# Other durations in the planner that orders attention, the entry of the output projection and the entry of the feed forward

## The chip, the cores and the metric

One core of a Trainium2 chip runs the whole kernel. The metric is the device time of one execution in microseconds (us), from three runs. Engines are named as in the profile: PE is TensorE (PEld its weight loads), DVE is VectorE, ACT is ScalarE, POOL is GpSimd, SP issues DMAs.

## The reference

One step of a backbone over 512 latent tokens (a grid of 8 x 64) and 128 context tokens of width 2048, all in float32:

```
m = silu(cond) @ w_ada + b_ada                      # shift, scale, gate, twice
h = rms_norm(x) * (1 + scale) + shift
q, k, v, u = split(h @ w_in)                        # 8 heads x 128 for q, k, v; 1024 for u
attn = softmax(q_n . [k_n in an 8 x 16 window + bias ; all 256 cached keys]) @ [v ; cached v]   # latent
attn = softmax(q_n . k_n) @ v                                                                   # context
pool = (window mean(u, 2/4/8/16) - u) @ w_pool * pool_scale
x = x + gate * concat(rms_norm(attn), rms_norm(pool)) @ w_out
h = rms_norm(x) * (1 + scale) + shift
x = x + gate * (silu(h @ w_gate) * (h @ w_up)) @ w_down
```

q_n and k_n are RMS-normalised per head. The outputs are both x and the context's k_n and v.

## The kernel before, in words

**Products.** Every large product is made of 256 x 256 blocks of weights, multiplied with seven products where the plain way has eight (a Strassen-Winograd form). The 640 tokens are two halves of 320 (`HB`; 322, `HX`, in the feed forward, where two columns carry the shift). One operand is a pair of 128-row tiles of activations, the other a 256 x 256 block of weights; of each, four given quarters and sums of them make seven tiles. Each tile is split into a high part (`hi`, rounded to the format that PE takes at full rate) and a low part (`lo`, the rest), so one of the seven products is three matmuls (lines 415 to 417). A **step** is one block of weights against one operand: 7 x 3 matmuls. Eight steps fill seven PSUM banks, and `combine` (lines 422 and 423; the first instruction is a ScalarE copy) adds them into an output block.

**What a step needs.** Its block of weights is fetched (`fetch`, line 336), its sums are made by three subtractions or additions (`sums`, line 342: 128, 128 and 256 columns), ScalarE copies the seven tiles to `hi` (`x_hi`, line 351), and a subtraction gives `lo` (`x_lo`, line 357, 896 columns). The operand of activations needs the same once: sums (`y_sum`, line 376: 640, 320 and 320 columns), copies to `hi` on ScalarE (lines 387 and 394), and subtractions for `lo` (line 389, 960 columns; line 396, 640 columns, twice).

**Who sets the order.** In most of the kernel the order stands in the loops (`step`): sums on GpSimd, `lo` on VectorE. In three stretches a planner sets it: the first block of the input projection, attention with the first block of the output projection, and the last block of the output projection with the first block of the feed forward. Code there records operations with `op` or `on`; each has a key (when it is wanted), a list of what it needs, the buffers it takes, and a duration for each engine that may do it. `issue` then lists them: it keeps a clock for each engine, computes for each operation that can be placed when it could start, takes the engine with the least start plus weighted duration, and among all that could start within a small window of the earliest places the one with the least key. The order in which operations are placed is the order in which each engine's instructions stand in the program; the engines wait for each other by semaphores, so the planner's clock is not seen at run time. The durations come from

```
    COST = {"ACT": (0.15, 0.83e-3), "DVE": (0.08, 1.05e-3), "Pool": (0.15, 2.1e-3)}
    ...
            fixed, each = (0.15, 0.65e-3) if copy and e == "DVE" else COST[e]
            alts[e] = fixed + each * n
    ...
                    (max(t, clock.get(e, 0.0)) + d * (1.0 + WEIGHT.get(e, 0.0)), max(t, clock.get(e, 0.0)), e)
```

(lines 530 to 540 and the choice in `issue`; `n` is the number of columns, the result is in us), and `STEP = 2.83` is the duration of a step on PE and the distance between the keys of two steps. `WEIGHT` makes VectorE and ScalarE count dearer in that choice than their durations say; the change leaves it alone.

**Attention** (lines 853 to 1476) records eight heads of five query blocks each. A block's chain is: scores on PE (lines 1069 to 1072), bias added on VectorE in PSUM (1080; the bias itself, masked, is made by line 1056 on VectorE or GpSimd), maximum (1093, 1094, VectorE), exponential (1100, ScalarE), reciprocal (1112, VectorE), transposes (1117, PE), a copy out of PSUM (544 ScalarE or 546 VectorE), values (1127, PE), a scaled copy (544 or 548). Beside it run the pooled features (`plan_features`, lines 1225 to 1249, elementwise on VectorE or GpSimd; products at 1269; their squares added at 1302), copies of x (1442), and the eight operands of the output projection: four of the pooled features (scaled at 1367) and, once all heads are done, four of attention (the sum over heads at 1397, its power at 908, a diagonal at 912, a row at 1329, scaled at 1419).

**The entry of the feed forward** (lines 1600 to 1730) records the last block of the output projection, the update of x (1507), its squares (1526, 552, 554, added at 1519 and 1627), the row of its norm (1329), and the eight operands of the feed forward.

Of the kernel before, what the change touches and what calls it, by code (L numbers as in the profile page):

```python
# [49 lines left out]
def tile_hybrid_step(  # L50
# [36 lines left out]
    def pool(name, **kw):  # L87
        cm = tc.tile_pool(name=name, bufs=1, reuse_waits="tile", **kw)
        return cm, cm.__enter__()
# [12 lines left out]
    def c_tile(i):  # L102
        return cp.tile([P, 2 * HX], F32, tag=f"c{i}", name=f"c{i}", bufs=1)
# [356 lines left out]
    def kind(name, n, make, begin=0.0):  # L460

        makers[name], held[name] = make, [begin] * n
# [4 lines left out]
    def op(eng, dur, key, fn, after=(), uses=(), lat=0.0):  # L467

        o = SimpleNamespace(eng=eng, dur=dur, key=key, fn=fn, after=[a for a in after if a], uses=uses, lat=lat, end=None)
        for b in uses:  # L470
            b.users.append(o)
        plan.append(o)
        return o
# [6 lines left out]
    def issue(begin=None, window=0.25):  # L480

        clock = dict(begin or {})
        taken.clear()
        plan.sort(key=lambda o: o.key)
        while plan:
            ready = []
            for o in plan:
                if any(a.end is None for a in o.after):
                    continue
                t = max([0.0] + [a.end + HOP for a in o.after])  # L490
                wanted = {}
                for b in o.uses:
                    if b.tile is None:
                        wanted.setdefault(b.kind, []).append(b)
                for k, bs in wanted.items():
                    t = max(t, sorted(free_at(h) for h in held[k])[len(bs) - 1])
                if t > 1e8:
                    continue
                alts = o.eng if isinstance(o.eng, dict) else {o.eng: o.dur}
                _, t, eng = min(  # L500
                    (max(t, clock.get(e, 0.0)) + d * (1.0 + WEIGHT.get(e, 0.0)), max(t, clock.get(e, 0.0)), e)
                    for e, d in alts.items()
                )
                ready.append((t, o, wanted, eng, alts[eng]))
            first = min(r[0] for r in ready)
            t, o, wanted, eng, dur = min((r for r in ready if r[0] <= first + window), key=lambda r: r[1].key)
            for k, bs in wanted.items():
                for b in bs:
                    i = min(range(len(held[k])), key=lambda i: free_at(held[k][i]))
                    held[k][i] = b  # L510
                    b.tile = makers[k](i)
            o.fn(eng) if isinstance(o.eng, dict) else o.fn()
            clock[eng] = t + dur
            o.end = t + dur + o.lat
            plan.remove(o)
# [16 lines left out]
    COST = {"ACT": (0.15, 0.83e-3), "DVE": (0.08, 1.05e-3), "Pool": (0.15, 2.1e-3)}  # L532
# [23 lines left out]
    STEP = 2.83  # L556
# [289 lines left out]
    def slot_tile(i, part, dtype):  # L846
        hop = hopA if i < 4 else hopB
        return hop.tile([P, 7 * HX], dtype, tag=f"{part}{i}", name=f"y{part}{i}", bufs=1)
# [3 lines left out]

    att_cm, att = pool("att")
    ps_cm, psum = pool("att_ps", space=PSUM)
    LEAD = 10.0

    att_kinds = set()

    def sb_kind(name, shape, n):
        att_kinds.add(name)  # L860
        kind(name, n, lambda i: att.tile(shape, F32, tag=f"{name}{i}", name=f"{name}{i}", bufs=1), LEAD)

# [28 lines left out]
    for name, n in (("s", 2), ("tp", 2), ("o", 1), ("x", 3), ("y", 0)):  # L891
        att_kinds.add(name)
        kind(name, n, lambda i, name=name: psum.tile([P, 512], F32, tag=f"{name}{i}", name=name, bufs=1), LEAD)

# [33 lines left out]

    begin = op("none", 0.0, -99, lambda: None, (), (), LEAD)
    later = op("none", 0.0, -99, lambda: None, (), (), 60.0)  # L930
# [258 lines left out]
    work = [[slot_tile(i, n, F32) for n in ("hi", "lo")] for i in range(2)]  # L1189
    kind("wk", 2, lambda i: work[i], LEAD)  # L1190
    SH = EXT + EXP
# [241 lines left out]
    kind("xi", 1, lambda i: c_tile(1)[:, 0:512])  # L1433
    kind("xo", 1, lambda i: c_tile(3)[:, 0:512], LEAD + 9)

# [54 lines left out]
    WEIGHT.update(DVE=1.6, ACT=0.5)  # L1490
    issue({e: LEAD for e in ("PE", "ACT", "DVE", "Pool")}, 0.05)
    c = [c_tile(q) for q in range(2)]
# [500 lines left out]
```

## Time and profile before

| what | us |
|---|---|
| median of 3 runs (2791.48 to 2798.62) | 2794.66 |
| the profiled execution | 2795.32 |
| its span, first to last instruction | 2793.1 |
| busy in the span: PE / DVE / ACT / POOL | 2616.0 / 1882.4 / 1087.4 / 1970.8 |
| from the last combine of the input projection to the first of the output projection | 569.65 to 807.00 |
| from the sixth further combine to the first of the feed forward | 968.41 to 1066.38 |

The profiled execution's time is 2.2 us above its span. An engine's busy time is from the start to the end that the record of an instruction shows, so time in which a running instruction is held up counts as busy. "Idle before" names what ended an engine's wait. A granted clock of 1.0 is PE's upper level (2.4 GHz), 0.5 its lower (1.2 GHz).

### The profile page before, as it was taken

To read this page: it belongs to the slowest core of one execution; us is meant where nothing else is said; L and a number is where in the kernel's file an instruction comes from. 1 tells how busy PE (TensorE), PEld (TensorE's weight loads), DVE (VectorE), ACT (ScalarE), POOL (GpSimd) and SP (SyncE) were. 2 spreads that over 40 slices of the span, in tenths; PEclk is the share of its full clock that TensorE was granted. 3 is DMA by queue.
4 is the path that set the end of the run, shared out by engine and by line. 5 is a ranking of instruction groups with operands and counts; after the bars stand their busy time and mean duration, and the time that the engine had idled before them with its cause. 6 is when DMAs were issued, how large, how long until landed. Compare 5 with 4: busy or idle time off the path is not lost.

```text
span 2793.1 us, 46356 instructions
## 1 busy us (share of the span) xinstructions
PE 2616.0 (94%) x16936; PEld 2424.4 (87%) x16936; DVE 1882.4 (67%) x2578; ACT 1087.4 (39%) x1605; POOL 1970.8 (71%) x2244
## 2 busy tenths in 40 slices
PE   6998999988779968999999999999999899999998
PEld 2478888877679968998999999999999889999997
DVE  2486434358775697665777777777777667787776
ACT  3133223246533434343444444444444323333333
POOL 2255656657678877666888888888888646887874
PEclk9999999989989979999999999999999999999999
DMA  9935777677245444664344344443443775365353
GB/s 333 340 120 205 270 252 260 229 228 221 84 142 177 158 134 137 201 193 141 117 126 144 122 135 122 126 140 117 126 140 115 260 250 206 127 211 190 111 168 103
DMA packets 370677, 487.17 MB, mean 174 GB/s; under 512 B 22928, under 2 KB 286608, under 8 KB 369808
## 3 DMA queue, kind: packets, MB, share of 16 engines
q1 hardware_dynamic: 367280, 479.36, 52.5%
q10 hardware_dynamic: 3168, 4.85, 0.6%
q8 instruction: 133, 2.18, 0.3%
q14 instruction: 96, 0.79, 0.1%
HBM read 394.33 MB, written 89.78 MB: 173 GB/s over the span
## 4 chain that ended last, share of the span: by engine, by line
PE 61%; DVE 15%; DMA 9%; POOL 7%; issue 4%; ACT 3%; SPq 1%; ACTq 0%; DVEq 0%; POOLq 0%
PE pp L417 18%; PE pp L415 18%; PE pp L416 17%; POOL wf L342 5%; DVE xlo L357 3%; DMA wf<-in_w_down_dram 2%; DVE c L422 2%; PE x L758 2%; ACT xhi L351 1%; DMA raw<-in_w_in_dram 1%; DMA araw<-in_w_ada_dram 1%; DMA wf<-in_w_out_dram 1%; DMA wf<-in_w_gate_dram 1%; DVE wf L342 1%; DMA wf<-in_w_up_dram 1%
## 5 line engine op out<-in xcount | busy, mean ns | idle before, releaser
L342 POOL TENSOR_TENSOR wf<-wf 128x128 f32<-128x128 f32 (+1 forms) x2004 | 1669.2, 840 | 558.0 <-DMA wf<-in_w_down_dram 110.5
L415 PE MATMUL pp<-yhi,xhi 128*128 128x322 f32 (+1 forms) x4072 | 1282.7, 315 | 25.8 <-ACT c L423 7.1
L417 PE MATMUL pp<-yhi,xlo 128*128 128x322 f32 (+1 forms) x4072 | 1280.7, 315 | 19.5 <-DVE xlo L357 16.6
L416 PE MATMUL pp<-ylo,xhi 128*128 128x322 f32 (+1 forms) x4072 | 1271.0, 312 | 19.4 <-DVE ylo L396 8.4
L357 DVE TENSOR_TENSOR xlo<-wf,xhi 128x896 fp32r<-128x896 f32 x678 | 799.0, 1186 | 662.0 <-ACT xhi L351 650.2
L351 ACT CAST xhi<-wf 128x896 fp32r<-128x896 f32 x688 | 648.1, 943 | 1243.3 <-POOL wf L342 1104.8
L415 PEld LDWEIGHTS pp<-yhi,xhi 128*128 128x128 f32 x4072 | 776.4, 191 | 53.3 <-DVE c L422 12.9
L417 PEld LDWEIGHTS pp<-yhi,xlo 128*128 128x128 f32 x4072 | 775.9, 191 | 35.4 <-DVE xlo L357 29.7
L416 PEld LDWEIGHTS pp<-ylo,xhi 128*128 128x128 f32 x4072 | 776.5, 191 | 21.7 <-DVE ylo L396 9.3
L422 DVE TENSOR_TENSOR c<-c,pp 128x320 f32<-128x320 f32 (+1 forms) x581 | 253.3, 483 | 43.6 <-ACT c L423 27.9
L415 PE MATMUL pp<-hhi,xhi 128*128 128x320 f32 x384 | 123.4, 321 | 4.4 <-DVE v L691 4.4
L417 PE MATMUL pp<-hhi,xlo 128*128 128x320 f32 x384 | 119.9, 312 | 1.0 <-DVE xlo L357 1.0
L416 PE MATMUL pp<-hlo,xhi 128*128 128x320 f32 x384 | 119.7, 312 | 0.0
L160 POOL TENSOR_TENSOR wlo<-raw,whi 128x512 fp32r<-128x512 f32 x32 | 42.9, 1363 | 85.0 <-ACT whi L159 85.0
L415 PEld LDWEIGHTS pp<-hhi,xhi 128*128 128x128 f32 x384 | 72.9, 190 | 23.4 <-issue 13.4
L415 PE MATMUL pp<-thi,xhi 128*128 128x320 f32 x288 | 90.3, 313 | 3.1 <-DVE c L422 1.9
L416 PE MATMUL pp<-tlo,xhi 128*128 128x320 f32 x288 | 90.4, 314 | 2.1 <-DVE tlo L653 2.1
L417 PE MATMUL pp<-thi,xlo 128*128 128x320 f32 x288 | 90.1, 313 | 0.0
L417 PEld LDWEIGHTS pp<-hhi,xlo 128*128 128x128 f32 x384 | 72.8, 190 | 1.7 <-DVE xlo L357 1.7
L416 PEld LDWEIGHTS pp<-hlo,xhi 128*128 128x128 f32 x384 | 73.0, 190 | 0.0
L691 DVE TENSOR_TENSOR v<-g,v 128x512 f32<-128x512 f32 x70 | 46.9, 684 | 37.0 <-PE g L166 37.0
L165 PE MATMUL g<-wlo,hhi 128*128 128x512 f32 x160 | 64.8, 405 | 5.5 <-POOL wlo L160 5.3
(249 smaller groups left out, 2624.6 us busy)
## 6 DMA issues: line engine op xcount, KB each, us to landing
araw<-in_w_ada_dram SPq DMA_DIRECT2D x60, 1024.0 KB, 6.5
wf<-in_w_gate_dram SPq DMA_DIRECT2D x176, 256.0 KB, 3.0
wf<-in_w_up_dram SPq DMA_DIRECT2D x176, 256.0 KB, 2.9
wf<-in_w_down_dram SPq DMA_DIRECT2D x176, 256.0 KB, 3.1
araw<-in_w_ada_dram SPq DMA_DIRECT2D x64, 512.0 KB, 6.9
wf<-in_w_in_dram SPq DMA_DIRECT2D x96, 256.0 KB, 4.4
yh_s<-yh SPq DMA_DIRECT2D x66, 320.0 KB, 3.6
wf<-in_w_out_dram SPq DMA_DIRECT2D x64, 256.0 KB, 2.8
```

The costliest lines, as they stand in the source:

```text
L160: nc.gpsimd.tensor_tensor(lo, raw, hi.bitcast(F32), op=ALU.subtract)
L165: mm(out, lhsT=xhi, rhs=wlo, start=False, stop=False)
L342: tt = lambda o, a, b, op: eng.tensor_tensor(o, a, b, op=op)
L351: nc.scalar.copy(hi, raws[s][:, 0:7, :])
L357: eng.tensor_tensor(lo, f[:, 0:7, :], hi.bitcast(F32), op=ALU.subtract)
L415: mm(b, lhsT=x[0][:, i, :], rhs=y[j][0], start=first, stop=False)
L416: mm(b, lhsT=x[0][:, i, :], rhs=y[j][1], start=False, stop=False)
L417: mm(b, lhsT=x[1][:, i, :], rhs=y[j][0], start=False, stop=last)
L422: add = lambda o, a, b: nc.vector.tensor_tensor(o, a, b, op=ALU.add)
L691: nc.vector.tensor_tensor(dst, ps, dst, op=ALU.add)
L758: mm(acc[32 * i : 32 * i + 32, :], lhsT=c4[:, k + i, :], rhs=raw[i], start=k == 0, stop=k == NKT - 4, tile_position=(0, 32 * i),)
```

## The change

Two lines stand at the start of attention, after the first planned stretch has been issued, so they hold for the two other stretches.

```
     att_cm, att = pool("att")
     ps_cm, psum = pool("att_ps", space=PSUM)
+    COST.update(ACT=(0.23, 0.8e-3), DVE=(0.2, 1.5e-3), Pool=(0.35, 2.2e-3))
+    STEP = 3.09
     LEAD = 10.0
```

For 640 columns the planner counts 1.16 us on VectorE (before: 0.75), 1.76 us on GpSimd (1.49) and 0.74 us on ScalarE (0.68). The durations of a copy on VectorE stay. No operation is added or left out. What moves is which engine does an operation and where it stands. Lines from 855 on have numbers higher by two in the changed kernel. Up to attention, in the blocks of the output projection between the two stretches, and behind the entry of the feed forward the order is as before.

The counts below are from the order of the two built programs: elementwise instructions on VectorE that read two tensors from SBUF (lines 342, 357, 376, 389, 396, 912, 1056, 1242 to 1249, 1302, 1367, 1419, 1507, 1519, 1627), and all instructions on GpSimd, with the sum of their columns. "Heads" runs from the start of attention to the sum over heads (line 1397), "tail" from there to the last `lo` of an operand of the output projection, "entry" from the combine in front of the last block of the output projection to the last `lo` of an operand of the feed forward.

| stretch | DVE before | DVE now | POOL before | POOL now |
|---|---|---|---|---|
| heads | 69, 27,716 columns | 56, 17,164 | 124, 37,277 | 124, 40,149 |
| tail | 35, 17,280 | 37, 18,944 | 22, 11,781 | 34, 18,437 |
| entry | 80, 38,718 | 78, 31,778 | 51, 19,959 | 48, 24,851 |

In the heads, line 1056 goes from 6 on VectorE and 26 on GpSimd to 13 and 19; lines 1245 and 1249 go from 11 and 13 to 5 and 19; and of the scaled copies of line 544/548 into `at`, four go from VectorE to ScalarE (29 and 11 before, 33 and 7 now). Of the four pooled operands of the output projection, before, three are fully split when line 1397 is reached and the fourth lacks two instructions of its `lo`; now one is fully split, a second lacks two instructions, and of the two others the scaling or the sums are unfinished too. In the entry, three sums of weights (line 342) go from GpSimd to VectorE, and two `lo` of weights (357), two of line 389 and four of line 396 go the other way; one more sum of weights, before on GpSimd, now stands behind the stretch.

**GpSimd behind the heads.** First the order before, from the power of the attention row on (`small`): one `lo` of a pooled operand is left (`ylo_7137`), then come the first scaled attention operand (`f_7165`) and its sums.

```order
L908 TENSOR_TENSOR small<-small,nhalf 128x5
L396 TENSOR_TENSOR ylo_7137<-f_7141,yhi_7136 128x640
L1419 TENSOR_TENSOR f_7165<-f_7165,c_7183 128x640
L376 TENSOR_TENSOR f_7171<-f_7165 128x2x320
L389 TENSOR_TENSOR ylo_7227<-f_7165,yhi_7226 128x960
L357 TENSOR_TENSOR xlo<-wf,xhi 128x896
L376 TENSOR_TENSOR f_7288<-f_7178 128x2x320
L357 TENSOR_TENSOR xlo<-wf,xhi 128x896
```

Now, from the same instruction:

```order
L910 TENSOR_TENSOR small<-small,nhalf 128x5
L376 TENSOR_TENSOR f_7143<-f_7094,f_7143 128x320
L914 TENSOR_TENSOR c_7151<-ident,small 128x640
L389 TENSOR_TENSOR ylo_7155<-f_7094,yhi_7154 128x960
L396 TENSOR_TENSOR ylo_7155<-f_7143,yhi_7154 128x640
L376 TENSOR_TENSOR f_7208<-f_7147,f_7208 128x320
L389 TENSOR_TENSOR ylo_7167<-f_7147,yhi_7166 128x960
L357 TENSOR_TENSOR xlo<-wf,xhi 128x896
L1421 TENSOR_TENSOR f_7211<-f_7211,c_7163 128x640
L357 TENSOR_TENSOR xlo<-wf,xhi 128x896
```

GpSimd makes the diagonal of the row itself (line 914, on VectorE before), and five instructions of two pooled operands (`f_7094`, `f_7147`) stand between the power and the first scaling of attention (line 1421).

**VectorE in the entry of the feed forward.** Before, from the update of x on (`c`, one of its two blocks), up to the next sum of weights (`wf`):

```order
L1507 SCALAR_TENSOR_TENSOR c_9527<-c_9527,g1c,xT 128x512
L1507 SCALAR_TENSOR_TENSOR c_9527<-c_9527,g1c,xT 128x128
L357 TENSOR_TENSOR xlo<-wf,xhi 128x896
L1627 TENSOR_TENSOR c_7614<-c_7614,xT 128x640
L396 TENSOR_TENSOR ylo_9544<-f_9541,yhi_9543 128x644 x2
L389 TENSOR_TENSOR ylo_9626<-f_9579,yhi_9625 128x966
L1627 TENSOR_TENSOR c_7614<-c_7614,xT 128x640
L376 TENSOR_TENSOR f_9631<-f_9579,f_9631 128x322
L342 TENSOR_TENSOR wf<-wf 128x128 x2
L342 TENSOR_TENSOR wf<-wf 128x256
```

Now:

```order
L1509 SCALAR_TENSOR_TENSOR c_9510<-c_9510,g1c,xT 128x512
L1509 SCALAR_TENSOR_TENSOR c_9510<-c_9510,g1c,xT 128x128
L342 TENSOR_TENSOR wf<-wf 128x128 x2
L342 TENSOR_TENSOR wf<-wf 128x256
L389 TENSOR_TENSOR ylo_9599<-f_9561,yhi_9598 128x966
L396 TENSOR_TENSOR ylo_9526<-f_9528,yhi_9525 128x644
L376 TENSOR_TENSOR f_9633<-f_9561 128x2x322
L1629 TENSOR_TENSOR c_7614<-c_7614,xT 128x640
L342 TENSOR_TENSOR wf<-wf 128x128 x2
L342 TENSOR_TENSOR wf<-wf 128x256
```

VectorE makes sums of weights here and leaves the long `lo` of the weights (line 357), one of the two additions of squares and one `lo` of an operand to GpSimd.

## Rows read from the trace of the kernel before

**Rows 1.** The page's busy time, share and instructions of each engine.

```profile
PE 2616.0 (94%) x16936; PEld 2424.4 (87%) x16936; DVE 1882.4 (67%) x2578; ACT 1087.4 (39%) x1605; POOL 1970.8 (71%) x2244
```

**Rows 2.** Timeline of ACT: start, duration, instruction; the first instruction of six combines.

```profile
569.65 0.43 ACT L423 COPY c<-pp 128x320 f32<-128x320 f32 x1 [1.93 <-PE pp L417]
...
807.00 0.43 ACT L423 COPY c<-pp 128x320 f32<-128x320 f32 x1
...
942.02 0.41 ACT L423 COPY c<-pp 128x320 f32<-128x320 f32 x1
...
968.41 0.42 ACT L423 COPY c<-pp 128x320 f32<-128x320 f32 x1
...
1017.62 0.42 ACT L423 COPY c<-pp 128x320 f32<-128x320 f32 x1
...
1066.38 0.43 ACT L423 COPY c<-pp 128x322 f32<-128x322 f32 x1 [0.54 <-PE pp L417]
```

**Rows 3.** Windows: length; busy PE, PEld, DVE, ACT, POOL; granted clock; DMA share, GB/s.

```profile
569.65:756.07 186.42, 155.40 (x984) 129.68 (x982) 143.85 (x327) 112.88 (x234) 124.35 (x127) 0.93 0.64 185
756.07:807.50 51.43, 30.87 (x155) 27.25 (x155) 43.46 (x38) 16.48 (x18) 36.63 (x23) 0.74 0.30 100
968.41:1066.38 97.97, 65.31 (x345) 61.20 (x344) 91.01 (x103) 40.22 (x55) 73.43 (x53) 0.81 0.40 128
```

**Rows 4.** Waits of 572 to 752 us: total, times, longest.

```profile
ACT pr L1100 <- DVE st L1094: 17.3, 19, 3.6
...
POOL bm L1056 <- DVE s L1080: 8.7, 7, 3.3
...
PE tp L1117 <- ACT pr L1100: 8.3, 7, 2.0
```

**Rows 5.** Timeline of DVE and POOL from 763 us: start, duration, instruction.

```profile
763.39 2.92 DVE L1419 TENSOR_TENSOR f<-f,c 128x640 f32<-128x640 f32 x2
763.53 2.10 POOL L1419 TENSOR_TENSOR f<-f,c 128x640 f32<-128x640 f32 x1 [3.79 <-DVE c L546]
765.70 2.06 POOL L376 TENSOR_TENSOR f<-f 128x640 f32<-128x640 f32 x1
...
767.72 2.25 POOL L389 TENSOR_TENSOR ylo<-f,yhi 128x960 fp32r<-128x960 f32 x1
767.79 2.53 DVE L376 TENSOR_TENSOR f<-f,f 128x320 f32<-128x320 f32 x1 [1.49 <-POOL f L376]
```

**Rows 6.** Lines from 572 to 812 us: count, least/median/most ns, first and last start.

```profile
L357 DVE TENSOR_TENSOR xlo<-wf,xhi x7: 1066/1083/1622, 573.6 to 811.3; 128x896 fp32r<-128x896 f32 x7
...
L357 POOL TENSOR_TENSOR xlo<-wf,xhi x3: 2112/2367/2702, 769.9 to 807.5; 128x896 fp32r<-128x896 f32 x3
...
L396 POOL TENSOR_TENSOR ylo<-f,yhi x8: 1529/1554/2192, 724.5 to 805.3; 128x640 fp32r<-128x640 f32 x8
L396 DVE TENSOR_TENSOR ylo<-f,yhi x8: 814/1350/2699, 736.0 to 805.3; 128x640 fp32r<-128x640 f32 x8
...
L376 DVE TENSOR_TENSOR f<-f,f x10: 478/493/2526, 720.1 to 803.4; 128x320 f32<-128x320 f32 x10
L376 POOL TENSOR_TENSOR f<-f,f x6: 866/1330/1793, 717.8 to 789.4; 128x320 f32<-128x320 f32 x6
```

**Rows 7.** The chain of work that ended last, 748 to 815 us: start, duration, what.

```profile
756.07 0.21 DVE small L1397
...
758.26 2.16 DVE c L912
760.47 2.52 PE x L1329 x4
763.00 0.30 DVE c L546
...
806.26 1.24 POOL ylo L396
```

More of the change, by code (lines that the diff above doesn't have):

```diff
@@ L854, in tile_hybrid_step @@
     ps_cm, psum = pool("att_ps", space=PSUM)
+    COST.update(ACT=(0.23, 0.8e-3), DVE=(0.2, 1.5e-3), Pool=(0.35, 2.2e-3))
+    STEP = 3.09
     LEAD = 10.0
```

## The prediction

> **What bounds the kernel now.** The page's busy line [rows 1] makes TensorE look like the bound, but it averages over the whole span, and the change touches two stretches only. I read those next, by the first instruction of each combine [rows 2]. An undisturbed block of the output projection takes 968.41 - 942.02 = 26.4 us. Attention with its first block takes 807.00 - 569.65 = 237.4 us. The entry of the feed forward, two blocks, takes 1066.38 - 968.41 = 98.0 us, 49.2 for the first and 48.8 for the second; two undisturbed blocks would take 53. So in both stretches PE is starved, by some 45 us in the entry.
>
> By windows [rows 3], in the entry VectorE shows 91.0 us busy of 98.0 and GpSimd 73.4. In the tail (756.07 to 807.5) they show 43.5 and 36.6 of 51.4, PE 30.9 at a granted clock of 0.74, which lies between its two levels. In the heads all are loaded: PE 155.4, VectorE 143.9 and GpSimd 124.4 of 186.4. The waits there [rows 4] run in a ring: ScalarE's exponential waits for VectorE's maximum (17.3 us), GpSimd for buffers that VectorE frees (8.7), PE for the exponential (8.3).
>
> What "busy" hides stands in the timeline [rows 5]. The GpSimd multiplication that starts at 763.53 takes 2.10 us, and the least for 640 columns is 1.53 [rows 6]; it ends at 765.63. VectorE's two multiplications of 640 columns in the same time take 2.92 us together instead of 2 x 0.81, and end at 766.31, 0.7 us behind GpSimd's end. At 767.79 VectorE starts 320 columns that alone take 0.48 us; the record is 2.53 us long and ends 0.35 us behind the GpSimd instruction that began at 767.72. So an instruction of VectorE that reads two tensors from SBUF and one of GpSimd take turns. I call what they take turns on the pair. From the least durations [rows 6], for n columns, VectorE holds it about 0.15 us + 1.03 ns x n (0.48 for 320, 0.81 for 640, 1.07 for 896), GpSimd about 0.18 us + 2.13 ns x n (0.87, 1.53, 2.11). **The same work holds the pair nearly twice as long on GpSimd.**
>
> With these two prices and the counts of the table on the change, the work on the pair before is:
>
> - entry: 80 x 0.15 + 38,718 x 1.03 ns = 51.9 on VectorE and 51 x 0.18 + 19,959 x 2.13 ns = 51.7 on GpSimd, 103.6 us, in a stretch of 98.0;
> - tail: 23.1 + 29.1 = 52.1 us, in 51.4;
> - heads: 38.9 + 101.7 = 140.6 us, in 186.4.
>
> Tail and entry are full of it; the sum even exceeds the time by 6% in the entry, so a little of each instruction lies beside its neighbour. The pair, and not either engine, sets these two stretches.
>
> **The change part by part.** No operation is added or removed; ScalarE takes four scaled copies of 128 columns more in the heads and has 73 us free there [rows 3], so this costs nothing while that slack lasts. The DMAs are the same, moved with their operations; attention's DMA share is 0.64 and the entry's 0.40 [rows 3], so I cost their places at nothing, and the bound on that is one late landing of a few us, inside the ranges below. What the new durations do is move two-input work between the engines, and this is costed by stretch.
>
> *Entry.* VectorE's share falls to 78 x 0.15 + 31,778 x 1.03 ns = 44.4 us (-7.5), GpSimd's rises to 48 x 0.18 + 24,851 x 2.13 ns = 61.6 us (+9.9). The pair has 106.0 us where it had 103.6: +2.4, and at the rate seen (98.0 / 103.6 = 0.946) +2.3 us. From below, if VectorE's own queue (91.0 of 98.0 us busy) were the bound, its 7.5 us would go. I take +2.3, since the pair is fuller than VectorE.
>
> *Tail.* VectorE gets 25.1 us (+2.0), GpSimd 45.4 us (+16.3): in the heads two pooled operands are left undone and pass to the tail. The pair has 70.5 us where it had 52.1, +18.4. Not all of it shows. Before, from the sum over heads at 756.07 to the row's last copy at 763.3 [rows 7], the chain is the power, the diagonal, the row on PE and a copy, and the pair does only some 3.4 us of work in 7.2 us (two halves of one `lo`, 0.81 and 1.53, and the diagonal). The other 48.7 us of its work take the 44.2 us to 807.5, a rate of 0.91. Now there is work to fill the 7.2 us (7.9 us of it at that rate), and the remaining 62.5 take 56.8: the tail is 64.0 us, +12.6. Its end is as before the last `lo` of the last operand [rows 7], so PE cannot start the last of its eight steps earlier. From above the whole 18.4 shows; from below, if only GpSimd's own record counted, it is 36.6 + 16.3 = 52.9 us against 51.4, +1.5. I take +12.6.
>
> *Heads.* VectorE's share falls to 26.1 us (-12.8), GpSimd's rises to 107.8 (+6.1): the pair has 6.7 us less. Here neither pair nor engine is full, so the price must be bounded. From above the heads shorten by nothing, if PE and the latency of the ring [rows 4] hold them. From below VectorE's recorded time is what goes: `lo` of 640 columns has a median of 1.35 us where the least is 0.81 [rows 6], so 12.8 us undisturbed are about 21 recorded, of 143.9. I take -7, close to what the pair saves, because the longer records are waits for the pair, and those do not go where GpSimd holds it longer.
>
> The sum is +12.6 + 2.3 - 7 = +7.9 us. The profiled execution took 2795.3 us, 0.7 above the median of the runs; so 2803.2 against it, **2802.5** against the median. About 0.3%, or 8.4 us, is what a measurement here can tell from no change, so this lies just inside.
>
> The Trainium skill ("SBUF — State Buffer", section "SBUF: two separate sides") says that VectorE with two SBUF inputs and GpSimd hold their shared ports as "an exclusive lock, not a bandwidth split", for the whole instruction. The timeline agrees on the turns [rows 5], but 103.6 us of work in 98.0 us speaks for a little overlap. Taken strictly, by that rule, the sum would be that of the second rival below.
>
> **The rivals.**
>
> *Faster: VectorE's queue bounds the heads.* The softmax's maxima and bias additions stand in one queue with elementwise work that is held up; 13 such instructions leave, and ScalarE's longest wait is for that queue [rows 4]. If the heads shorten by the recorded 21 us, the sum is 12.6 + 2.3 - 21 = -6 us, 2789. It decides once the heads shorten by more than 14.9 us; by more than 23 it can be measured. Against it: what stays on VectorE is held up longer by a busier GpSimd, and PE is the fullest engine there.
>
> *Slower: the turns leave no overlap.* Then the sums count in full: +18.4 + 2.4 - 6.7 = +14.1 us, 2809. For it, the tail's 52.1 us in 51.4; against it, the entry's rate.
>
> *Slower: the heads do not shorten,* since PE, 155.4 of 186.4 us busy, and the ring set them: 12.6 + 2.3 = +14.9 us, 2810.
>
> *Faster: each engine's own record counts, not the pair.* Heads -21, tail +1.5, entry -7.5: -27 us, 2768. The alternation of the timeline speaks against it. The same side would be reached if durations closer to the records (the planner's 1.16 us for 640 columns against a median of 1.35 [rows 6]; before it counted 0.75) let the order wait less all over.
>
> That the change does nothing is ruled out by the order: both stretches differ on every engine.
>
> **How the numbers follow.** Forecast 0.42, the queue of VectorE 0.22, no overlap 0.10, heads not shorter 0.14, own records or an order that fits better 0.12. Around the forecast the bounds reach from 2796 to 2810, and about half of that lies beyond +8.4 us. Slower: 0.20 of the forecast, 0.09 and 0.11 of the two slower rivals, together 0.40. Faster: 0.08 of VectorE's queue and all of the last, together 0.20. The same: 0.40. The range leaves out most of the last rival and the far end of the slower ones: 2783 to 2815.
>
> **What would show it.** In the new profile the tail, from the sum over heads to the last `lo`, should grow from 51.4 to about 64 us, with GpSimd's busy time there up by 16 or more; the heads should shrink from 186.4 to about 179; the entry should stay within 2 or 3 us of 98.0, with less VectorE time and more GpSimd time. VectorE's additions that lie beside GpSimd work should still show records that end 0.3 to 0.9 us behind GpSimd's. The prediction is wrong if the tail grows by under 5 us with these counts, if the entry falls with VectorE's share, or if the heads shorten by 15 us or more.

## The result, and the profile after

The changed kernel takes **2813.26 us** (median of 7 runs, 2802.88 to 2815.99), the kernel before 2794.66 (7 runs on the same chip). The ratio is 1.006, 95% interval 1.0047 to 1.0072: slower by 13 to 20 us. The profiled execution took 2810.63 us, its span is 2808.8. The page's busy line, which answers to [rows 1], hides where:

```profile
PE 2633.3 (94%) x16936; PEld 2438.8 (87%) x16936; DVE 1878.0 (67%) x2567; ACT 1087.3 (39%) x1604; POOL 1987.1 (71%) x2256
```

GpSimd has 16 us more, VectorE 4 less, and PE 17 more for the same 16936 products. The windows of the changed kernel show the place; they run as in [rows 3] from the first instruction of a combine to the sum over heads (heads), from there to the next combine (tail), and over the two blocks of the entry. Columns: length; busy PE, PEld, DVE, ACT, POOL; granted clock; DMA share, GB/s.

```profile
569.57:759.30 189.73, 165.49 (x984) 138.51 (x982) 127.92 (x309) 109.92 (x233) 121.89 (x127) 0.88 0.64 182
759.30:822.90 63.60, 34.80 (x155) 29.90 (x155) 52.16 (x41) 20.55 (x21) 55.08 (x34) 0.73 0.25 82
983.97:1086.67 102.70, 70.80 (x351) 64.22 (x349) 92.63 (x106) 38.80 (x51) 76.54 (x53) 0.80 0.39 123
```

Against [rows 3] the heads took 3.3 us more, the tail 12.7 more (63.6; before 50.9 up to the combine at 807.00 of [rows 2]), the entry 4.7 more. Together that is 20.7 us. What lies between tail and entry and behind it took 1883.2 us, before 1888.1, so the span grew by 15.7.

In the tail the alternation of [rows 5] fills more time. The timeline of VectorE and GpSimd in the tail of the changed kernel (start, duration, instruction):

```profile
799.63 4.71 DVE L342 TENSOR_TENSOR wf<-wf 128x128 f32<-128x128 f32 x3
...
801.93 2.12 POOL L357 TENSOR_TENSOR xlo<-wf,xhi 128x896 fp32r<-128x896 f32 x1
...
804.02 1.71 POOL L396 TENSOR_TENSOR ylo<-f,yhi 128x640 fp32r<-128x640 f32 x1
804.26 2.48 DVE L389 TENSOR_TENSOR ylo<-f,yhi 128x960 fp32r<-128x960 f32 x1
805.69 2.46 POOL L376 TENSOR_TENSOR f<-f 128x640 f32<-128x640 f32 x1
...
806.66 2.17 DVE L396 TENSOR_TENSOR ylo<-f,yhi 128x640 fp32r<-128x640 f32 x1
...
822.21 2.12 POOL L396 TENSOR_TENSOR ylo<-f,yhi 128x640 fp32r<-128x640 f32 x1
```

VectorE's three sums end at 804.34, 0.3 us behind the GpSimd instruction that ends at 804.05; its 960 columns end 1.0 us behind 805.73, its 640 columns 0.7 behind 808.15. They are records of waiting, as before: the 640 columns took 2.17 us where the least is 0.81 [rows 6]. The last line is the tail's last `lo`; it ends at 824.33, 65.0 us behind the sum over heads.

In the heads other waits are long now. The waits of 572 to 752 us of the changed kernel (total, times, longest):

```profile
ACT at L544 <- PE o L1129: 22.7, 24, 2.4
DVE s L1082 <- PE s L1072: 15.2, 14, 3.1
POOL bm L1058 <- DVE s L1082: 12.2, 8, 2.4
...
ACT pr L1102 <- DVE st L1096: 5.2, 5, 2.3
```

Two of the same waits in the kernel before, which [rows 4] leave out:

```profile
ACT at L544 <- PE o L1127: 12.9, 18, 1.5
...
DVE s L1080 <- PE s L1070: 4.6, 7, 1.7
```

ScalarE's wait for VectorE's maximum fell from 17.3 us [rows 4] to 5.2, as the rival on VectorE's queue would have it. In its place VectorE waits for PE's scores (15.2 us; before 4.6) and ScalarE for PE's sums of values (22.7; before 12.9). A second execution of each kernel shows the same shifts: 15.7 before to 6.4 for the maximum, 5.7 to 12.5 for the scores, 14.0 to 22.8 for the sums of values.

### The profile page after: what moved, and what is told of

The parts are those of the page before. It is cut to its first block, busy times and chain, and to the rows that moved or that the text cites. A ratio compares the mean times of both kernels' runs of the same rounds, so it can differ in the third digit from the quotient of the medians.

```text
span 2808.8 us, 46353 instructions
## 1 busy us (share of the span) xinstructions
PE 2633.3 (94%) x16936; PEld 2438.8 (87%) x16936; DVE 1878.0 (67%) x2567; ACT 1087.3 (39%) x1604; POOL 1987.1 (71%) x2256
## 4 chain that ended last, share of the span: by engine, by line
PE 41%; DVE 9%; POOL 6%; DMA 4%; issue 3%; ACT 2%; SPq 0%; ACTq 0%; DVEq 0%; POOLq 0%
PE pp L417 13%; PE pp L415 13%; PE pp L416 13%; POOL wf L342 5%; DVE xlo L357 3%; DVE c L422 2%; DMA wf<-in_w_down_dram 1%; ACT xhi L351 1%; DMA wf<-in_w_gate_dram 1%; DMA wf<-in_w_up_dram 1%; DVE cx L422 1%; PE x L758 1%; DVE wf L342 1%; DVE c L1684 1%; DVE c L1657 0%
## 5 line engine op out<-in xcount | busy, mean ns | idle before, releaser
L415 PEld LDWEIGHTS pp<-hhi,xhi 128*128 128x128 f32 x384 | 73.3, 191 | 23.0 <-issue 10.9
```

The source lines that it names most:

```text
L415: mm(b, lhsT=x[0][:, i, :], rhs=y[j][0], start=first, stop=False)
```

## The experiments

All stand against the kernel before on the same chip. Work on the pair is counted from the order at the prediction's prices.

**One part at a time.** First the new durations only for the entry, two lines ahead of its recording:

```
+    COST.update(ACT=(0.23, 0.8e-3), DVE=(0.2, 1.5e-3), Pool=(0.35, 2.2e-3))
+    STEP = 3.09
     T_BLK = STEP * NKP
```

> The new durations hold for the entry of the feed forward alone; attention is planned as before. Theory of the turns (VectorE with two SBUF inputs and GpSimd share one pair, and a stretch lasts as long as its work on it): attention stays at 237.4 us from combine to combine, the entry has 106.0 us of pair work instead of 103.6 and takes 100 to 103 us instead of 98.0; in all +2 to +5 us over before. Rival (each engine's own queue counts, and VectorE with 91 us busy of 98 bounds the entry): the entry falls by up to 7 us with VectorE's share, so -7 to 0 us.

2804.08 us, ratio 1.0026 (1.0014 to 1.0038). The whole is some 7 us slower, more than the 2 to 5 expected. Windows of the heads and the entry:

```profile
570.46:760.20 189.74, 159.16 (x984) 133.12 (x982) 145.18 (x326) 113.02 (x234) 122.61 (x127) 0.92 0.62 182
...
972.13:1075.59 103.46, 70.01 (x351) 62.33 (x349) 91.81 (x106) 38.80 (x50) 76.37 (x53) 0.82 0.39 122
```

The entry has the 103 us of the changed kernel; VectorE, which has 7.5 us less of pair work there, is busy 91.8 us where it was 91.0 [rows 3]. The heads, whose order on every engine is that of before, took 3.3 us more than in [rows 3] as well: one profile of the heads does not settle a term of that size.

Then only for attention (the change, with the old values set again ahead of the entry):

```
+    COST.update(ACT=(0.15, 0.83e-3), DVE=(0.08, 1.05e-3), Pool=(0.15, 2.1e-3))
+    STEP = 2.83
     T_BLK = STEP * NKP
```

> The new durations hold for attention and the first block of the output projection alone; the old ones are set again before the entry of the feed forward is planned. Turns: attention 253 us from combine to combine as in the changed kernel (tail 63 to 64 us with 70.5 us of pair work, heads 189 to 190), the entry 98 us; in all +14 to +17 us over before. Rival (the loss is in the entry, or in what follows from it): under +6 us.

2809.15 us, ratio 1.0046 (1.0031 to 1.006). The tail's window:

```profile
761.20:824.90 63.70, 35.62 (x155) 30.76 (x155) 52.24 (x40) 20.52 (x22) 55.00 (x34) 0.71 0.25 82
```

The tail repeats the changed kernel's (63.7 us); the heads took 187.3, and the entry stayed at 97.9. The whole is some 13 us slower, a little under the 14 to 17 expected. The parts add up to 0.72%, against 0.6% for the whole.

**The step alone.**

```
     ps_cm, psum = pool("att_ps", space=PSUM)
+    STEP = 3.09
```

> Only the step of 3.09 us, with the old durations of the engines. Pair work by the order: heads 140.6 us as before, tail 52.0 (before 52.1), entry 98.5 (before 103.6). Turns: attention within 2 us of before, the entry 98.5 x 0.946 = 93 us, in all -5 us, or -3 to -7. Rival (the distance between the keys of the steps, not the engines' durations, spoils the order): +10 us or more, most of what the change cost.

2799.69 us, ratio 1.0016 (1.0004 to 1.0027). Windows of heads and entry:

```profile
572.60:765.90 193.30, 164.76 (x984) 138.54 (x982) 145.12 (x327) 112.98 (x234) 123.02 (x128) 0.87 0.61 178
...
979.34:1074.82 95.48, 67.02 (x351) 63.29 (x349) 90.15 (x114) 39.14 (x52) 59.59 (x40) 0.79 0.41 129
```

Longer steps alone take work off the pair in the entry (103.6 to 98.5 us), and it shortens to 95.5; the tail has the same 52 us on the pair and takes 49.5. So the longer step alone does not lengthen them; the new durations without it were not run. The whole is still some 4.5 us slower, where 3 to 7 us faster was expected. The heads of this profile took 193.3 us with the order of before and a granted clock of 0.87; whether that is the loss was not settled.

**The other direction.** GpSimd twice as dear, from the start of attention:

```
     ps_cm, psum = pool("att_ps", space=PSUM)
+    COST.update(Pool=(0.3, 4.2e-3))
```

> The old durations, but GpSimd counted twice as dear (0.3 us and 4.2 ns a column), so the planner gives VectorE the work that the change gave GpSimd. Pair work by the order: heads 108.8 us (before 140.6), tail 39.3 (52.1), entry 87.2 (103.6). Turns: the tail 40 to 44 us instead of 51.4, the entry 82 to 87 us instead of 98.0, the heads within 5 us of before since PE sets them; in all -15 to -30 us. Rival (each engine's own queue counts): VectorE, the busiest engine of tail and entry before, gets 10 us more in the entry and 5 in the tail, and 31 in the heads, so tail and entry grow by 5 to 10 us and the heads by 10 or more: +20 us.

2786.11 us, ratio 0.9966 (0.9954 to 0.9978). Windows of heads, tail, entry:

```profile
571.86:766.50 194.64, 160.98 (x984) 133.81 (x982) 153.98 (x386) 115.81 (x243) 70.11 (x61) 0.91 0.61 177
766.50:810.23 43.73, 30.57 (x154) 27.64 (x154) 37.00 (x43) 15.51 (x16) 20.43 (x17) 0.77 0.38 125
970.45:1058.36 87.91, 61.88 (x351) 57.88 (x349) 82.23 (x116) 39.98 (x54) 40.57 (x35) 0.84 0.44 140
```

Tail and entry shorten with the pair's work, though VectorE does more of it. The entry has 87.2 us on the pair. The tail has 45.0 up to its last `lo`, counted from the trace (42 instructions and 24,128 columns on VectorE, 17 and 5,061 on GpSimd); the 39.3 of the expectation is too small. The heads have 32 us less on the pair, and do not shorten. So the whole gained only 9.5 us (6 to 13), where 15 to 30 were expected.

Then GpSimd out of tail and entry almost wholly, the heads left as they were:

```
     pool_ready = plan_operands(T_ALL * 1.0, *plan_pooling(T_ALL * 0.1, T_ALL * 0.12))
+    COST.update(Pool=(0.4, 1e-1))
```

> The order of before up to the sum over heads; from there on GpSimd's planned price is 0.4 us + 100 ns per column, so almost all two-input work of tail and entry goes to VectorE. Work on the pair by the order, at the two prices of the prediction: heads 140.6 us as before, tail 37.5 (before 52.1), entry 73.7 (before 103.6). Turns on the pair: the tail takes 40 to 44 us (before 50.9; PE's eight steps and the row limit it below that), the entry 76 to 84 (before 98.0; VectorE alone then has 70.4 us of pair work and some 8 us of other work in one queue), the heads stay within 4 us of 186.5: together -20 to -30 us, some 2765 to 2775 us. Each engine's own queue by its recorded time: VectorE, 91.0 us busy of 98.0 in the entry, gets 18.5 us more there and 12.6 more in the tail, so the entry takes 110 us or more and the tail 55 or more: +15 us or more.

2773.79 us (4 runs), ratio 0.9919 (0.989 to 0.9948): faster than both kernels. Its windows of heads, tail and entry:

```profile
572.10:761.20 189.10, 161.19 (x984) 134.63 (x982) 144.58 (x327) 112.69 (x234) 122.20 (x128) 0.90 0.63 182
761.20:799.60 38.40, 29.25 (x155) 26.37 (x155) 34.27 (x54) 16.10 (x18) 3.19 (x2) 0.79 0.34 112
961.37:1047.57 86.20, 62.10 (x351) 59.09 (x350) 79.09 (x140) 41.00 (x58) 7.80 (x8) 0.86 0.45 143
```

Its longest wait of ScalarE in the entry:

```profile
ACT xhi L351 <- DVE wf L342: 16.7, 7, 4.6
```

Its line of an operand's last `lo` in the entry (count, least/median/most ns, first and last start):

```profile
L396 DVE TENSOR_TENSOR ylo<-f,yhi x16: 819/821/825, 985.1 to 1042.7; 128x644 fp32r<-128x644 f32 x16
```

The same line in the entry of the kernel before, with PE's wait for it:

```profile
L396 DVE TENSOR_TENSOR ylo<-f,yhi x13: 822/1874/2604, 996.0 to 1065.6; 128x644 fp32r<-128x644 f32 x13
...
  PE pp L416: 2.1, 1
```

And in the changed kernel:

```profile
L396 DVE TENSOR_TENSOR ylo<-f,yhi x9: 812/1351/2064, 1011.8 to 1086.0; 128x644 fp32r<-128x644 f32 x9
...
  PE pp L416: 10.9, 5
```

With GpSimd silent, all 16 instructions of VectorE take 0.82 us. Before, the median of the 13 on VectorE was 1.87. The tail, with 38.3 us on the pair in the trace, took 38.4, less than the 40 to 44 expected. The entry reached 86.2 us, not the 73.7 of the pair and a little over the expected range: VectorE is busy 79.1 of it and ScalarE waits 16.7 us for its sums of weights, which speaks for VectorE's own queue as the new bound; no run tests that.

**More work in the tail that nobody waits for.** GpSimd gets one addition behind each of its six subtractions:

```
+    def extra(eng, x):
+        if scratch and eng is nc.gpsimd:
+            eng.tensor_tensor(scratch[1], x, x, op=ALU.add)
...
             eng.tensor_tensor(op[1][:, part, :], s[:, part, :], op[0][:, part, :].bitcast(F32), op=ALU.subtract)
+            extra(eng, s[:, part, :])
```

> The order of before with six more GpSimd additions of 640 columns with two SBUF inputs in the tail, one behind each subtraction that GpSimd does for an operand once attention's buffers are closed; their result goes to a spare buffer and nobody waits for it. Five of them lie ahead of the last subtraction of the tail. Turns on the pair: 5 x 1.54 = 7.7 us of work more on the pair, which runs at a rate of 0.91 to 1, so the tail takes 58 to 59 us (before 50.9) although no operation of it waits for the additions. GpSimd's own queue: it is idle for 14.8 of the 51.4 us, so the tail takes 51 to 53.

2802.86 us, ratio 1.0023 (1.0009 to 1.0037). The tail's window:

```profile
764.20:819.96 55.76, 31.20 (x155) 27.68 (x155) 48.73 (x38) 16.08 (x18) 45.03 (x27) 0.72 0.25 82
```

The added line (count, least/median/most ns):

```profile
L374 POOL TENSOR_TENSOR scratch<-f x6: 1249/1460/1838, 778.1 to 820.5; 128x640 f32<-128x640 f32 x6
```

The timeline of the tail's end (lines from 369 on have numbers higher by six, from 389 on by seven):

```profile
812.23 1.43 POOL L374 TENSOR_TENSOR scratch<-f 128x640 f32<-128x640 f32 x1
812.47 1.87 DVE L403 TENSOR_TENSOR ylo<-f,yhi 128x640 fp32r<-128x640 f32 x1
814.26 0.81 DVE L382 TENSOR_TENSOR f<-f 128x640 f32<-128x640 f32 x1
...
815.11 0.49 DVE L382 TENSOR_TENSOR f<-f,f 128x320 f32<-128x320 f32 x1
...
815.52 1.08 DVE L357 TENSOR_TENSOR xlo<-wf,xhi 128x896 fp32r<-128x896 f32 x1
...
816.52 0.48 DVE L382 TENSOR_TENSOR f<-f,f 128x320 f32<-128x320 f32 x1
...
818.37 2.19 POOL L403 TENSOR_TENSOR ylo<-f,yhi 128x640 fp32r<-128x640 f32 x1 [4.72 <-ACT yhi L401]
```

Five additions, 7.6 us by their records, lie in the tail. It grew by 5.2 us over the 50.6 in the mean of six executions with the order of before, between the two expectations. VectorE's recorded time grew by 5.3 (from 43.46 [rows 3]) with no instruction added to it. The rest of the 7.6 fits gaps like the one that the timeline shows: the last addition ends at 813.66, GpSimd waits 4.7 us for ScalarE, and there VectorE's instructions take their least durations (0.81, 0.49, 1.08, 0.48). So the pair is not busy to the end. (How the rest of the 7.6 us divides over such gaps was not counted.)

VectorE gets two multiplications behind each of its six subtractions, in and out of PSUM:

```
+            for _ in range(2):
+                eng.tensor_scalar(scratch[0], scratch[0], 1.0, None, op0=ALU.mult)
```

> The order of before with twelve more VectorE multiplications in the tail, two behind each of the six subtractions that VectorE does for an operand once attention's buffers are closed, each on 512 columns of one spare PSUM bank, in and out, so that they touch no SBUF; nobody waits for them. At some 0.65 us each (a copy of 512 columns from PSUM took 0.68 us in the entry of before) they are 7 to 8 us of VectorE. Turns on the pair: they lie beside GpSimd's turns, as VectorE alone has some 25 to 28 us of work in the 51.4, so the tail takes 51 to 54 us. VectorE's own queue by its record (43.5 us busy of 51.4): it takes 57 to 59.

2800.89 us, ratio 1.0016 (1.0004 to 1.0028). The tail's window:

```profile
762.70:815.84 53.14, 33.64 (x155) 28.79 (x155) 45.97 (x49) 15.85 (x18) 36.09 (x22) 0.74 0.27 86
```

The added line:

```profile
L375 DVE TENSOR_SCALAR x<-x x12: 685/696/700, 783.1 to 816.6; 128x512 f32<-128x512 f32 x12
```

Ten of them, 6.9 us, lie in the tail, which grew by 2.5; none is ever held up (685 to 700 ns). VectorE's record grew by only 2.5 us too: the added work took the place of waiting. Per us of added work the pair's costs 0.7 by the records (0.8 if each of the five additions is counted at its least, 1.25 us), VectorE's own 0.4.

**How far the heads differ between executions.** Both kernels once more.

> The kernel before once more, for how far one stretch of one program differs between two executions. If the heads' length is set by the order, they take 186.5 us within 1 us, and the 189.7 of the run with this same order in the heads has another cause; if the granted clock there varies from run to run, they differ by 2 us or more, with the mean granted clock (0.93 before) lower where they are longer. Tail and entry within 1 us of 50.9 and 98.0 on either account.

The window of its heads (tail 50.2 us, entry 97.9):

```profile
570.34:758.70 188.36, 157.08 (x984) 130.40 (x982) 143.30 (x326) 112.87 (x234) 123.97 (x127) 0.93 0.62 183
```

The heads are 1.9 us longer than in the first profile at the same mean clock, which decides for neither account.

> The changed kernel once more, for how far its stretches differ between two executions. Tail 63.6 and entry 102.7 us within 1 us, as the order sets them; heads between 186 and 192 us, where those of six executions with the order of before lay, on the account that the change leaves the heads' length as it was; 187 or less twice in two would speak for a small gain in the heads, 192 or more for a loss.

The changed kernel's windows of heads, tail and entry in this execution:

```profile
568.83:752.10 183.27, 159.28 (x984) 133.54 (x982) 128.24 (x309) 110.02 (x233) 122.38 (x128) 0.92 0.65 188
752.10:815.51 63.41, 34.73 (x155) 29.82 (x155) 52.08 (x40) 20.42 (x21) 54.71 (x34) 0.73 0.25 82
976.53:1079.80 103.27, 73.44 (x351) 65.86 (x349) 92.39 (x106) 38.87 (x50) 75.28 (x53) 0.77 0.39 122
```

Tail and entry repeat within 0.8 us. The changed kernel's heads took 183.3 us here and 189.7 in the first profile, the same program. With the order of before (seven executions, those of e1, e3, e5, e6, e7 among them) they took 186.4 to 193.3, mean 190.0; with the changed order (three) 183.3 to 189.7, mean 186.8. So the gain is 3 us in the mean, and the two ranges overlap. These executions ran on several chips, which may add to the spread.

**What the heads wait for.** Each engine in turn gets some 9 to 11 us more in the order of before.

```
-        powed = op("Pool", 1.95, key, lambda: power(b.r.tile[:, 0:10], 10), (aff,), (b.r,))
+        def raised():
+            power(b.r.tile[:, 0:10], 10)
+            nc.gpsimd.tensor_tensor(spare, b.k.tile, b.k.tile, op=ALU.mult)
+
+        powed = op("Pool", 1.95, key, raised, (aff,), (b.r, b.k))
```

> The order of before with one more GpSimd multiplication of 640 columns with two SBUF inputs for each of the eight heads, behind the head's power on GpSimd; its result goes to a spare buffer and nobody waits for it. That is 8 x 1.54 = 12.3 us more on the pair in the heads, 140.6 to 152.9. Over six executions with the order of before the heads took 186.4 to 191.7 us, 189.5 in the mean. The heads' term of the prediction (pair work there costs about its own time): 200 to 203 us. PE and the latency of the ring hold the heads, not the pair: GpSimd is idle for 62 of 186 us, so 189 to 194 us.

```
+        def inverse():
+            nc.vector.reciprocal(b.r.tile[:, 10:15], b.r.tile[:, 5:10])
+            for _ in range(2):
+                nc.vector.tensor_scalar(spare, b.k.tile, 1.0, None, op0=ALU.mult)
...
-            key, 5, lambda: nc.vector.reciprocal(b.r.tile[:, 10:15], b.r.tile[:, 5:10]), (powed,), (b.r,)
+            key, 5, lambda: inverse(), (powed,), (b.r, b.k)
```

> The order of before with two more VectorE multiplications of 640 columns by a constant (one SBUF input, one SBUF output) for each head, behind the head's reciprocal; the result goes to a spare buffer and nobody waits for it. At 0.6 to 0.75 us each, worked out from 0.38 us for 320 columns, that is 10 to 12 us of VectorE, whose recorded busy time in the heads is 143.9 of 186.4 us. VectorE's queue bounds the heads (first rival of the prediction): 198 to 202 us. PE and the ring: 190 to 194. If a VectorE instruction with one SBUF input takes turns with GpSimd as well, its records beside GpSimd work are 1.5 us or longer instead of 0.75.

```
-                lambda row=row, c0=c0, c1=c1: mm(
-                    row.tile[:, 0 : c1 - c0], lhsT=ones, rhs=b.diag.tile[:, c0:c1], start=True, stop=True
-                ),
+                lambda row=row, c0=c0, c1=c1: [
+                    mm(row.tile[:, 0 : c1 - c0], lhsT=ones, rhs=b.diag.tile[:, c0:c1], start=True, stop=True)
+                    for _ in range(2)
+                ],
```

> The order of before with each head's row of reciprocal norms for the keys multiplied out twice into the same bank: 16 products of 512 columns and 16 of 128 more on PE in the heads, 9.2 + 3.3 = 12.5 us by the rows of before. PE, 155.4 to 162 us busy of 189.5, sets the heads with its queue: 199 to 203 us. The ring of waits sets them (PE starved in each turn, so that more work fits beside the waits): 190 to 195 us. If the granted clock rises with PE's work, the other products get faster and the heads stay at 189 with a mean clock above 0.93.

The window of the heads with more on GpSimd:

```profile
571.21:762.20 190.99, 158.44 (x984) 133.01 (x982) 146.38 (x327) 113.35 (x234) 134.88 (x136) 0.92 0.62 180
```

Its added line:

```profile
L986 POOL TENSOR_TENSOR spare<-k x8: 1248/1254/1445, 583.7 to 727.7; 128x640 f32<-128x640 f32 x8
```

The window of the heads with more on VectorE:

```profile
572.36:768.40 196.04, 164.15 (x984) 136.87 (x982) 154.59 (x342) 112.99 (x234) 121.99 (x128) 0.90 0.60 176
```

Its added line:

```profile
L988 DVE TENSOR_SCALAR spare<-k x16: 445/1035/1742, 585.6 to 734.2; 128x640 f32<-128x640 f32 x16
```

The window of the heads with more on PE:

```profile
567.47:756.90 189.43, 164.11 (x1016) 135.00 (x1014) 145.07 (x327) 113.34 (x234) 124.21 (x127) 0.94 0.63 182
```

GpSimd: 191.0 us, whole 2799.49 us, 1.0011 (1.0001 to 1.0021). VectorE: 196.0 us, whole 2802.48, 1.002 (1.0009 to 1.003). PE: 189.4 us at a granted clock of 0.94, whole 2802.3, 1.0015 (1.0002 to 1.0029). By the windows only the heads with more on VectorE lie outside the 186.4 to 193.3 us of the seven executions without added work, and those multiplications are held up by GpSimd too (last section), so that run does not tell VectorE's queue from the pair. PE's record grew by 8.7 us over [rows 3], not by the 12.5 expected; that the heads then took 189 us at a clock of 0.94 is the third outcome named in the expectation, but two executions without the doubled products had 0.93.

By the whole times 10 us more on GpSimd cost about 3 us (0.3 to 6), the 10.7 us by which VectorE's record grew about 5.6 (2.5 to 8.4), the doubled products about 4 (0.6 to 8). None shows in full, and the intervals overlap, so which engine comes nearest to setting the heads is not shown. Nor can so small a difference be put down to one stretch: with the step alone tail and entry were 3.5 us shorter, and the whole 4.5 us longer.

## Why the prediction was off by 11 us

The time lies in the range of 2783 to 2815, 11 us above the forecast of 2802.5. By step:

**Turns on the pair, and the tail (+12.6): right.** The tail was forecast at 64.0 us to its last `lo`; it took 65.0, 65.1 and 64.8 in three executions, against 51.4 to 51.5 in six with the order of before (to the first instruction of the combine, as in the windows, 63.6, 63.7 and 63.4 against 50.1 to 51.1). GpSimd's busy time there rose by 18 us, the sign that was forecast. The least and held-up durations of one line with GpSimd silent and busy show the mechanism itself. Stretches against the work on the pair (us; where several executions share an order, their range):

| tail: pair | measured | entry: pair | measured |
|---|---|---|---|
| 38.3 (e5) | 38.4 | 73.7 (e5) | 86.2 |
| 45.0 (e4) | 43.7 | 87.2 (e4) | 87.9 |
| 52.0 (e3) | 49.5 | 98.5 (e3) | 95.5 |
| 52.1 (before) | 50.1 to 51.1 | 103.6 (before) | 97.4 to 98.2 |
| 70.5 (after) | 63.4 to 63.7 | 106.0 (after) | 102.7 to 103.5 |

The tails of e4 and e5 have about the columns of before on the two engines together (29,189 and 28,549, before 29,061), only more of them on VectorE. The changed tail has 37,381 (table of the change), because pooled operands came over unfinished from the heads. So its 18.4 us more on the pair are two things. As an estimate at the prediction's prices, the 14 instructions and 8,320 columns by which it grew would hold the pair 10.7 us on VectorE; the rest of the 18.4 is that most of them went to GpSimd.

**The entry (+2.3): sign right, size wrong.** It took 97.9 us in the mean of eight executions with its order of before and 103.1 in three with the new one: +5.3, outside the 2 or 3 us that were named as a sign. The step that failed is the fixed rate, 98.0 / 103.6 = 0.946 us of stretch per us of pair. The table has rates from 0.94 to 1.01 for the entry, e5 aside. How much of the pair's work lies in gaps depends on the order: in the changed entry PE waited 10.9 us for the `lo` of line 396 (11.0 and 7.7 in two more executions of that order), before 2.1. That this makes up the other 3 us is argued, not shown. VectorE's share fell by 7.5 us and the entry did not follow, so the bound from below, VectorE's queue, is refuted here.

**The heads (-7): the step that failed.** It priced pair work in the heads at about its own time. In e4 32 us less of it shortened nothing (VectorE's record rose by 10 us there, though), and with 10 us more on GpSimd in e9 the heads took 191.0 us, inside the range without it. What the mean of the executions leaves is a gain of 3 us. Whether the gain is 3 us or none stays open, as the same program differs by 6.5 us there, and what sets the heads instead was not found. The third rival (heads not shorter, 2810) came nearest.

**The sum.** By the stretches the change costs 13.0 + 5.3 - 3.3 = 15.0 us, inside the 13 to 20 measured. The three terms missed by 0.4, 3.0 and 3.7 us, all to the same side; that is 7.1 of the 11 us, and the rest lies within the interval of the measurement. That the time lies in the range does not bear out the heads' term.

**The rivals.** VectorE's queue did give way in the heads, as ScalarE's wait suggests, and VectorE's recorded time there fell by 16 us; but waits for PE took their place, and the heads did not shorten by the 14.9 us from which that rival decides. Turns without overlap would have made the tail +18.4; +13.0 refutes that. Each engine's own record, the planner's view too, is refuted most plainly by e5: with 18.5 us more pair work VectorE's record in the entry fell from 91.0 to 79.1 us.

So the new durations, nearer to the records, lengthened the kernel: a record on VectorE holds its waiting for GpSimd. For 640 columns the planner's price went from 0.75 to 1.16 us on VectorE and from 1.49 to 1.76 on GpSimd, and so it moved work to the engine that holds the pair longer, and some of it from the heads to the tail, where the pair was full.

## What to carry to other kernels

Before a planner's duration is corrected to the recorded one, look at whether the record holds a wait: compare the least duration of the line with its median, and see whose end the long ones follow. Where two engines share something, add up what both hold of it in the stretch; the sum, and not either engine's busy time, is what a move of work changes. A stretch that is a ring of short waits takes several executions of either kernel before a term of a few us there can be told.

## What was not expected of the hardware

**One input is enough.** The prediction's rule spoke of VectorE instructions with two inputs in SBUF. The multiplication of e10 has one, and its output is in SBUF: it took 0.445 us for 640 columns at best and 1.742 at most. Its timeline:

```profile
600.59 1.26 POOL L913 TENSOR_TENSOR diag<-ident,r 128x640 f32<-128x640 f32 x1
...
600.67 2.06 DVE L988 TENSOR_SCALAR spare<-k 128x640 f32<-128x640 f32 x2
```

GpSimd's instruction ends at 601.85, and the two on VectorE at 602.73, 0.88 us later, about twice 0.445. Taken singly, the first ends 0.35 us behind GpSimd's end, and the second then takes 0.49 with GpSimd idle. Seven of the 16 took 1.4 to 1.7 us, each beside GpSimd's work. The Trainium skill ("SBUF — State Buffer", section "Who interferes with whom") says that VectorE's copies and multiplications by a scalar can run in a mode that takes the ports shared with GpSimd, while an instruction with at most one SBUF input outside these modes does not contend. The runs agree as far as they go: 445 to 1742 ns here, 685 to 700 ns for the one of e7, which stays in PSUM and has no SBUF input. In which mode an instruction ran, the trace does not show.

**The heads and the granted clock.** In the executions with one order the heads are the longer, the lower the mean granted clock, with one exception: before, 186.4 us at 0.93 and 193.3 at 0.87 (between them 188.4, 189.7, 191.6, 191.7 and 189.1 at 0.93, 0.92, 0.91, 0.90 and 0.90); changed, 183.3, 187.3 and 189.7 at 0.92, 0.90 and 0.88. These are means between the clock's two levels, 1.2 and 2.4 GHz (0.50 and 1.00). At about the same clock the changed heads were some 2 to 6 us shorter. Which is cause and which effect was not tried.
